# A recurrent mixer's scan in stages between the weight tiles of the next pair's products, with its GpSimd work on other engines

## The chip, the cores and the metric

The kernel runs on one core of one Trainium2 chip. The core has five engines that work side by side, each through its own queue in order: TensorE (PE in the profile, its weight loads PEld), VectorE (DVE), ScalarE (ACT), GpSimd (POOL) and SyncE (SP), which here only issues DMAs. The metric is the device time of one execution in microseconds (us); lower is better.

## The reference

One layer of a decoder with 256 tokens and a width of 2048, in float32: half a SwiGLU step, a token mixer with two branches (attention and a gated linear recurrence, HGRN2), and another half SwiGLU step. Only the recurrent branch is touched here:

```python
def hgrn2_branch(hq, hf, hi, hg, lower_bound, out_norm, w_o):
    q = heads(jax.nn.silu(hq), HGRN_EXPAND)
    f_gate = lb + (1.0 - lb) * jax.nn.sigmoid(hf)
    k = heads(1.0 - f_gate, HGRN_EXPAND)
    log_f = heads(jnp.log(f_gate), HGRN_EXPAND)
    v = heads(hi, HGRN_HEAD_DIM)
    ...
    def step(state, inp):            # a chunk of 64 tokens
        qc, kc, vc, gc = inp
        b = jnp.cumsum(gc, axis=2)
        inter = jnp.einsum('bhtk,bhkv->bhtv', qc * jnp.exp(b), state)
        ...
        scores = jnp.einsum('bhtk,bhtsk,bhsk->bhts', qc, decay, kc)
        intra = jnp.einsum('bhts,bhsv->bhtv', scores, vc)
        ...
        return new_state, inter + intra
    ...
    o = rmsnorm(o, out_norm) * jax.nn.silu(hg)
    return o @ w_o
```

The decay between tokens s and t is the product of the forget gates f from s+1 to t, in each of 128 features; there are 16 heads of 128 features.

## The kernel before

The time goes into matrix products with large weights. Weights come from memory in tiles of 128x1024 (`fetch`, L81), all on SP's queue. `load_w` (L86) makes two parts of each, a rounded one `whi` (ACT, L95) and the rest `wlo` (DVE, L96), so that products of float32 come out as sums of fast ones. There are four buffers each of `raw`, `whi` and `wlo`, so both engines may work up to four tiles ahead of PE. `gemm_t` (L99) gives 256 columns transposed and takes 16 products from a tile (L111 to L115, alternately 512 and 256 columns wide); `gemm_n` (L130) gives 512 columns by tokens and takes 12 products from a tile (L126 to L128, each 512 wide).

The recurrent mixer, `hgrn` (L599 on), works on eight pairs of heads. For each pair `pair_in` (L623) makes q, f and k from two products of four tiles each, and `values_in` or `gates_in` (L653, L660) makes, for two pairs at a time, the values or the output gates from a product of eight tiles. So a pair has sixteen weight tiles. Beside them stands the `scan` (L673) of the pair before. It replaces the chunked recurrence by doubling: `pre` holds products of f from the start of a block, `suf` products to the end of a block, and `double` (L705) makes blocks twice as long, `suf` on POOL (L706) and `pre` on DVE (L707). At block lengths 8, 16, 32 and 64 the scores between the two halves of a block are a small product (L741, two a level) of A = q x pre (L735) and B = k x suf (L737), both from DVE; blocks of 8 are done at once, with reciprocals (L719, L720) and the products of L728. Masked copies on DVE (L711) or copies on ACT (L747, L748) put the scores into `sT`. A last product (L754) couples the two halves of the tokens. `heads_out` (L759) multiplies scores and values (L764 to L766), norms and gates the result, and `merge` (L782) turns it (L785) and splits it into `ob`, the operand of the branch's output product.

The tile framework's scheduler sets the order on each engine. It takes the instructions in the order in which the program writes them, by readiness and its own estimates, and writes a fixed queue for each engine; within a queue nothing overtakes. The program writes a whole scan in one piece behind the last product of the next pair, `heads_out` and `merge` at two points of the pair after that (`step` at L640 and L642). After the last pair two products of the branch's output gate, `gate_b` (`fill`, L818, L820), stand between the last scans and outputs; the other six follow, one ahead of each output product.

Of the kernel before, what the change touches and what calls it, by code (L numbers as in the profile page):

```python
# [37 lines left out]
# Where the next operand's transposes stand in program order, along the product that runs beside them (see gemm_n), and  # L38
# by how many instructions the rest of that operand's chain is put ahead; columns of the residual at a time.
# [21 lines left out]
class Ops:  # L61
    """Pools and the pieces that the stages share."""
# [36 lines left out]
    def gemm_t(self, w, act, kt):  # L99
        """256 weight columns, result transposed: a bank for 128 columns, [column, token] in two addends."""  # L100
        nc = self.nc
        ps = self.mm.tile([P, 2, 512], F32, name="mm")
        for g in range(kt // 4):
            hi, lo = self.load_w(w[g])
            for i in range(4):
                k = g * 4 + i
                for j in range(2):
# [5 lines left out]
                    else:  # L113
                        nc.tensor.matmul(ps[:, j, 0:T], lo[:, c], both[:, 0], start=False, stop=False)  # L114
                        nc.tensor.matmul(ps[:, j], hi[:, c], both, start=False, stop=k == kt - 1)  # L115
# [14 lines left out]
    def gemm_n(self, w, act, kt, n=512, late=0, pool=None, own=0, hooks=()):  # L130
# [15 lines left out]
        for g in range(kt // kg):  # L146
# [3 lines left out]
            for i in range(kg):  # L150
# [21 lines left out]
    def rstd_of(self, ssq, n, width, half=False):  # L172
        """ssq [P, n] sums of squares -> 1 / sqrt(mean + eps), or half of it."""
# [20 lines left out]
    def transposed(self, src, act, c, tt):  # L194
        """split(transpose(src)) into the k-tiles 4c.. of act."""
# [10 lines left out]
    def prenorm(self, x, ssq, wname, act, tt, ws=None):  # L206
        """act = split(transpose(x * rstd * w)) for half of the tokens."""
# [10 lines left out]
    def weighted(self, ps, c, z, wname):  # L218
        """z = y * w, a quarter of the columns."""
# [3 lines left out]
    def residual(self, x, z, rstd, done):  # L223
        """x += rstd * z, some of the columns at a time."""
# [43 lines left out]
def layer_kernel(ctx, tc, a, out):  # L268
# [9 lines left out]
    def ffn(n, act, fp, x_src, x_dst, nxt, hooks=()):  # L278
# [3 lines left out]
        # the first columns by halves of the tokens  # L282
# [62 lines left out]
    def gate_b(c):  # L345
        pg = ops.gemm_t(a["w_gb"][c], h, KD)
# [17 lines left out]
    with tc.tile_pool(name="hgrn", bufs=1, reuse_waits="tile") as gp:  # L364
        hgrn(ops, gp, h, ob, lambda i: gts.append(gate_b(i)))
    with tc.tile_pool(name="mg", bufs=1, side="right", reuse_waits="tile") as mgp:
        mg = mgp.tile([P, 2, KD, T], F32R, name="mg")
# [531 lines left out]
```

## Time and profile before

| | us |
|---|---|
| time, median of 3 runs | 2565.45 (2565.07 to 2565.91) |
| the profiled execution, first to last instruction | 2564.2 |
| in which DVE is busy | 1477.7 |
| in which ACT is busy | 1186.9 |
| in which POOL is busy | 181.1 |
| POOL in six pairs of the recurrent mixer, 1210 to 1520 | 94.4 |

No other time of the profiled execution is given than its span. The mixer's first scan begins at about 1200 us, the last output is merged at about 1560 us. A row of the profile that groups instructions gives the line, the engine, what is written from what, the shape, the count, the busy time in all and the mean of one in ns, then the idle time before them with what ended it. In the profile the operand h of these products goes by the name `after`. A float32 product that is not split counts as two instructions (L741 stands as x4 for the two products of a level).

### The profile page before, as it was taken

Reading aid. Unit: us, or ns where it says so; the run is one execution under the profiler, and the core shown is the slowest. Engines: PE = TensorE matmul, PEld = TensorE weight load, DVE = VectorE, ACT = ScalarE, POOL = GpSimd, SP = SyncE. Lnnn points to the kernel's source line nnn. Section 1 sums busy time; section 2 is a strip of 40 time slices with the busy share of each in tenths; the row PEclk is TensorE's granted clock in tenths of the full one; section 3 lists DMA queues with packets and bytes.
Section 4 is the critical chain, followed back from the end, with each engine's and each line's share of the span. In section 5 each row is a group of like instructions: output and inputs, shape, how many; then the busy total and the mean of one; then the engine's idle time right before and its main releaser. Section 6 shows DMA issues by size and latency. Waiting matters only on the chain.

```text
span 2564.2 us, 33907 instructions
## 1 busy us (share of the span) xinstructions
PE 2521.4 (98%) x13316; PEld 2147.1 (84%) x13316; DVE 1477.7 (58%) x1732; ACT 1186.9 (46%) x1552; POOL 181.1 (7%) x181
## 2 busy tenths in 40 slices
PE   8999999999999999999999999999999999999998
PEld 6888888888878898888888888888788888888887
DVE  5555555544466666556777776555655555554444
ACT  5444444434344556444444444444544444443433
POOL 0000000000000100111323231120000000000000
PEclk9999999999999999999999999999999999999999
DMA  7555555556686444555545444567755555555655
GB/s 255 174 188 189 188 183 190 188 188 199 201 271 188 162 140 148 188 181 181 165 163 169 161 157 158 188 205 242 231 175 188 187 186 188 189 189 188 197 195 184
DMA packets 137248, 481.13 MB, mean 188 GB/s; under 512 B 15616, under 2 KB 16000, under 8 KB 136320
## 3 DMA queue, kind: packets, MB, share of 16 engines
q1 hardware_dynamic: 137088, 478.97, 57.3%
q8 instruction: 104, 1.70, 0.3%
q14 instruction: 56, 0.46, 0.1%
HBM read 472.61 MB, written 6.29 MB: 187 GB/s over the span
## 4 chain that ended last, share of the span: by engine, by line
PE 93%; DVE 3%; POOL 1%; issue 1%; DMA 1%; ACT 1%; SPq 0%; POOLq 0%; DVEq 0%; ACTq 0%
PE mm L115 34%; PE mm L114 18%; PE mm L126 11%; PE mm L127 11%; PE mm L128 11%; PE mm L111 2%; PE mm L112 1%; POOL suf L706 1%; PE tp L198 0%; DVE sT L711 0%; PE sp L534 0%; PE sp L533 0%; DVE wlo L96 0%; PE sp L728 0%; PE tp L565 0%
## 5 line engine op out<-in xcount | busy, mean ns | idle before, releaser
L96 DVE TENSOR_TENSOR wlo<-raw,whi 128x1024 fp32r<-128x1024 f32 x826 | 1024.8, 1243 | 763.5 <-ACT whi L95 762.3
L95 ACT CAST whi<-raw 128x1024 fp32r<-128x1024 f32 x826 | 865.7, 1050 | 891.2 <-PE mm L115 425.3
L115 PE MATMUL mm<-h,whi 128*128 128x512 f32 x2400 | 846.0, 393 | 0.0
L114 PE MATMUL mm<-h,wlo 128*128 128x256 f32 x2400 | 678.1, 283 | 0.0
L115 PEld LDWEIGHTS mm<-h,whi 128*128 128x128 f32 x2400 | 450.7, 188 | 100.7
L114 PEld LDWEIGHTS mm<-h,wlo 128*128 128x128 f32 x2400 | 451.2, 188 | 3.8
L115 PE MATMUL mm<-after,whi 128*128 128x512 f32 x960 | 340.1, 394 | 0.0
L114 PE MATMUL mm<-after,wlo 128*128 128x256 f32 x960 | 273.1, 284 | 0.0
L127 PE MATMUL mm<-wlo,at 128*128 128x512 f32 x664 | 262.0, 395 | 0.0
L126 PE MATMUL mm<-whi,at 128*128 128x512 f32 x664 | 262.0, 395 | 0.0
L128 PE MATMUL mm<-whi,at 128*128 128x512 f32 x664 | 261.7, 395 | 0.0
L115 PEld LDWEIGHTS mm<-after,whi 128*128 128x128 f32 x960 | 180.4, 188 | 38.9
L114 PEld LDWEIGHTS mm<-after,wlo 128*128 128x128 f32 x960 | 180.6, 188 | 1.2
L126 PEld LDWEIGHTS mm<-whi,at 128*128 128x128 f32 x664 | 125.1, 188 | 29.2
L128 PEld LDWEIGHTS mm<-whi,at 128*128 128x128 f32 x664 | 125.1, 188 | 29.2
L127 PEld LDWEIGHTS mm<-wlo,at 128*128 128x128 f32 x664 | 125.1, 188 | 29.2
L178 POOL TENSOR_TENSOR rs<-ms,mhalf 128x1 f32<-128x1 f32 x16 | 9.7, 605 | 1633.3 <-DVE ms L176 1633.3
L126 PE MATMUL mm<-whi,after 128*128 128x512 f32 x304 | 120.9, 398 | 1.2 <-ACT after L164 1.2
L128 PE MATMUL mm<-whi,after 128*128 128x512 f32 x304 | 120.1, 395 | 0.0
L127 PE MATMUL mm<-wlo,after 128*128 128x512 f32 x304 | 120.0, 395 | 0.0
L115 PE MATMUL mm<-oa,whi 128*128 128x512 f32 x240 | 84.6, 393 | 0.0
L115 PE MATMUL mm<-ob,whi 128*128 128x512 f32 x240 | 84.6, 393 | 0.0
(276 smaller groups left out, 2860.9 us busy)
## 6 DMA issues: line engine op xcount, KB each, us to landing
raw<-in_ffn_w_gate SPq DMA_DIRECT2D x176, 512.0 KB, 4.3
raw<-in_ffn_w_up SPq DMA_DIRECT2D x176, 512.0 KB, 3.5
raw<-in_ffn_w_down SPq DMA_DIRECT2D x176, 512.0 KB, 4.3
raw<-in_w_ga SPq DMA_DIRECT2D x32, 512.0 KB, 3.4
raw<-in_mla_w_o SPq DMA_DIRECT2D x32, 512.0 KB, 3.6
raw<-in_w_hq SPq DMA_DIRECT2D x32, 512.0 KB, 3.6
raw<-in_w_hf SPq DMA_DIRECT2D x32, 512.0 KB, 3.5
raw<-in_w_hi SPq DMA_DIRECT2D x32, 512.0 KB, 3.5
```

The source lines that it names most:

```text
L95: nc.scalar.copy(out=hi, in_=raw)
L96: nc.vector.tensor_tensor(out=lo, in0=raw, in1=hi.bitcast(F32), op=ALU.subtract)
L111: nc.tensor.matmul(ps[:, j], hi[:, c], both, start=True, stop=False)
L112: nc.tensor.matmul(ps[:, j, 0:T], lo[:, c], both[:, 0], start=False, stop=False)
L114: nc.tensor.matmul(ps[:, j, 0:T], lo[:, c], both[:, 0], start=False, stop=False)
L115: nc.tensor.matmul(ps[:, j], hi[:, c], both, start=False, stop=k == kt - 1)
L126: nc.tensor.matmul(o, both[:, 0, r], hi[:, c], start=k == 0, stop=False)
L127: nc.tensor.matmul(o, both[:, 0, r], lo[:, c], start=False, stop=False)
L128: nc.tensor.matmul(o, both[:, 1, r], hi[:, c], start=False, stop=k == kt - 1)
L178: self.nc.gpsimd.tensor_tensor(out=r, in0=ms, in1=self.mhalf[:, 0:n], op=ALU.pow)
L706: G.tensor_tensor(out=part(suf, n, True), in0=part(suf, n, True), in1=ends(pre, n, False), op=ALU.mult)
```

## The change

The scan becomes a generator of eight stages, the outputs one of two. `gemm_t` and `gemm_n` call `tick` after each weight tile, and `tick` runs the stages that `lay` has planned for this place: those of a scan after every second tile of the next pair's sixteen, from the second tile on; those of the outputs after the third and the sixth. The last scan has one stage after each tile of the first two output gates, of which the mixer now takes three (`fill(2)`), so that five follow.

Each stage first issues the score products whose operands the stage before has made, then DVE's work for the next level. A and B of a level are made for both halves of the tokens by one operation each (before: two). POOL's operations move: `suf` goes to DVE, its first doubling as a copy to ACT; f = lb1 x sigmoid + lb and k = 1 - f go to ACT, the clamp of f to DVE. The norm's weight is no longer multiplied into the gates, but into the merge, where it is a scalar for each partition. The last doubling makes only the halves that are used.

```diff
-    def gemm_t(self, w, act, kt):
+    def gemm_t(self, w, act, kt, tick=None):
...
+            if tick:
+                tick()
...
     def pair_in(pr, tick):
...
         for j in range(2):
             c = slice(2 * pr + j, 2 * pr + j + 1)
-            G.tensor_scalar(out=f[:, :, j], in0=sf[:, :, j], scalar1=lb1[:, c], scalar2=lb[:, c], op0=ALU.mult,
-                            op1=ALU.add)
+            S.activation(out=f[:, :, j], in_=sf[:, :, j], func=AF.Identity, scale=lb1[:, c], bias=lb[:, c])
-        G.tensor_scalar(out=k, in0=f, scalar1=-1.0, scalar2=1.0, op0=ALU.mult, op1=ALU.add)
-        G.tensor_scalar(out=f, in0=f, scalar1=F_MIN, scalar2=None, op0=ALU.max)
+        S.activation(out=k, in_=f, func=AF.Copy, scale=-1.0, bias=1.0)
+        V.tensor_scalar(out=f, in0=f, scalar1=F_MIN, scalar2=None, op0=ALU.max)
...
     def gates_in(g, tick):
...
-        G.tensor_tensor(out=gv, in0=gv, in1=onw.unsqueeze(1).broadcast_to([P, 8, P]), op=ALU.mult)
...
         def double(n):
-            G.tensor_tensor(out=part(suf, n, True), in0=part(suf, n, True), in1=ends(pre, n, False), op=ALU.mult)
-            V.tensor_tensor(out=part(pre, n, False), in0=part(pre, n, False), in1=ends(pre, n, True), op=ALU.mult)
+            es, ls = (slice(0, 1), slice(1, 2)) if 2 * n == P else (slice(0, 2), slice(0, 2))
+            if n == 1:
+                S.copy(out=part(suf, n, True), in_=ends(pre, n, False))
+            else:
+                V.tensor_tensor(out=part(suf, n, True)[:, es], in0=part(suf, n, True)[:, es],
+                                in1=ends(pre, n, False)[:, es], op=ALU.mult)
+            V.tensor_tensor(out=part(pre, n, False)[:, ls], in0=part(pre, n, False)[:, ls],
+                            in1=ends(pre, n, True)[:, ls], op=ALU.mult)
...
         double(1)
         double(2)
+        yield
...
-        pick(0, ps)
-        double(4)
         for i, n in enumerate(LEVELS):
...
-            for tt in range(NT):
-                V.tensor_tensor(out=placed(A, n, tt, False), in0=halves(q, n, tt, False), in1=halves(pre, n, tt, False),
-                                op=ALU.mult)
-                V.tensor_tensor(out=placed(B, n, tt, True), in0=halves(k, n, tt, True), in1=halves(suf, n, tt, True),
-                                op=ALU.mult)
+            V.tensor_tensor(out=placed(A, n, False), in0=part(q, n, False), in1=part(pre, n, False), op=ALU.mult)
+            V.tensor_tensor(out=placed(B, n, True), in0=part(k, n, True), in1=part(suf, n, True), op=ALU.mult)
+            if i == 0:
+                pick(0, ps)
+            double(n)
+            yield
             ps = sp.tile([P, 2, 2, P], F32, name="sp")
...
-            double(n)
...
-            ops.split(ob[:, 0, 2 * pr:2 * pr + 2], ob[:, 1, 2 * pr:2 * pr + 2], o)
+        S.activation(out=hi, in_=o, func=AF.Copy, scale=onw)
+        V.scalar_tensor_tensor(out=lo, in0=o, scalar=onw, in1=hi.bitcast(F32), op0=ALU.mult, op1=ALU.subtract)
...
+    plan, left = [], []
+
+    def tick():
+        if plan:
+            for stage in plan.pop(0):
+                next(stage, None)
+
+    def lay(pairs):
+        for first, apart, gen in pairs:
+            for i in range(8 if gen.__name__ == "scan" else 2):
+                while len(plan) <= first + i * apart:
+                    plan.append([])
+                plan[first + i * apart].append(gen)
...
     for pr in range(8):
+        if pr > 1:
+            lay([(2, 3, outputs(*left.pop(0)))])
+        if pr:
+            lay([(1, 2, scanned(*pend))])
...
+    lay([(1, 2, outputs(*left.pop(0))), (0, 1, scanned(*pend))])
+    fill(0, tick)
+    fill(1, tick)
+    lay([(0, 2, outputs(*left.pop(0)))])
+    fill(2, tick)
```

The queues show what this moves. First PE's, before, where the scan of the third pair begins (L728 are the scores in blocks of 8, L741 those of a level, L111 and L112 the next pair's products):

```order
L128 MATMUL mm<-whi,after_4283 128x512
L728 MATMUL sp<-A_10937,B_10938 128x128 x4
L741 MATMUL sp<-A,B 128x128 x2
L111 MATMUL mm<-after_4283,whi 128x512
L112 MATMUL mm<-after_4283,wlo 128x256
L111 MATMUL mm<-after_4283,whi 128x512
L741 MATMUL sp<-A,B 128x128 x2
L112 MATMUL mm<-after_4283,wlo 128x256
```

The two first levels have three products between them, the next two come after 17 and 10 more, and the last small product (L754) after another 10; so the scan lies within the first product of a pair. The same place of the changed kernel, with the lines of that kernel (L735 for L728, L747 for L741, L792 the turn of the outputs, L116 and L117 for L114 and L115):

```order
L117 MATMUL mm<-after_4283,whi 128x512
L792 MATMUL tp<-ident,xn 128x128 x4
L735 MATMUL sp<-A_10661,B_10662 128x128 x4
L116 MATMUL mm<-after_4283,wlo 128x256
L117 MATMUL mm<-after_4283,whi 128x512
L116 MATMUL mm<-after_4283,wlo 128x256
```

Here 32 products stand between L735 and the first L747, and 24 from each small product to the next, so the scan lies over the whole pair.

Next DVE, before, behind the first reciprocal of the same scan (L735 and L737 are A and B, L707 is `pre`, L96 a weight tile's rest):

```order
L720 RECIPROCAL tmp<-f 128x2x32x4
L96 TENSOR_TENSOR wlo<-raw,whi 128x1024
L721 TENSOR_TENSOR A_10937<-q,tmp 128x2x32x4
L96 TENSOR_TENSOR wlo<-raw,whi 128x1024
L722 TENSOR_TENSOR A_10937<-q,f 128x2x32x4
L724 TENSOR_TENSOR B_10938<-k,tmp 128x2x32x4
L707 TENSOR_TENSOR f<-f 128x2x32x4
L737 TENSOR_TENSOR B<-k,suf 128x16x8
L735 TENSOR_TENSOR A<-q,f 128x16x8
L96 TENSOR_TENSOR wlo<-raw,whi 128x1024
L735 TENSOR_TENSOR A<-q,f 128x16x8
L737 TENSOR_TENSOR B<-k,suf 128x16x8
```

And now (L708 is `suf`, L710 `pre`, L739 and L740 are A and B):

```order
L725 RECIPROCAL tmp<-f 128x2x32x4
L96 TENSOR_TENSOR wlo<-raw,whi 128x1024
L726 TENSOR_TENSOR A_10661<-q,tmp 128x2x32x4
L728 TENSOR_TENSOR B_10662<-k,suf 128x2x32x4
L727 TENSOR_TENSOR A_10661<-q,f 128x2x32x4
L96 TENSOR_TENSOR wlo<-raw,whi 128x1024
L729 TENSOR_TENSOR B_10662<-k,tmp 128x2x32x4
L708 TENSOR_TENSOR suf<-suf,f 128x2x32x4
L710 TENSOR_TENSOR f<-f 128x2x32x4
L740 TENSOR_TENSOR B<-k,suf 128x2x16x8
L739 TENSOR_TENSOR A<-q,f 128x2x16x8
L96 TENSOR_TENSOR wlo<-raw,whi 128x1024
```

`suf` stands among DVE's own operations, and A and B of a level are one operation each. Ahead of these rows stand three doublings (L710, L708, L710) and the first reciprocal behind one wlo; behind them come six more scan operations (L708, L710, L740, L739, L708, L710), in every other pair the gate's product with them, and four wlo with hardly anything between.

Last the tail on DVE, in the last scan (L715 is a masked copy, L125 adds up an output gate, L796 is the merge):

```order
L715 COPY_PREDICATED sT<-masks,sp 128x512
L96 TENSOR_TENSOR wlo<-raw,whi 128x1024
L125 TENSOR_TENSOR gb<-gb,mm 128x512
L796 SCALAR_TENSOR_TENSOR ob<-tp,onw,ob 128x512
L715 COPY_PREDICATED sT<-masks,sp 128x512
L739 TENSOR_TENSOR A<-q,f 128x2x4x32
L740 TENSOR_TENSOR B<-k,suf 128x2x4x32
L96 TENSOR_TENSOR wlo<-raw,whi 128x1024
L715 COPY_PREDICATED sT<-masks,sp 128x512
L708 TENSOR_TENSOR suf<-suf,f 128x2x4x32
L96 TENSOR_TENSOR wlo<-raw,whi 128x1024
L710 TENSOR_TENSOR f<-f 128x2x4x32
```

Two operations of the outputs (L786, 128x256) stand ahead of these rows behind the same wlo; B and A of level 64 follow them, and on PE that level's product stands one tile earlier. One stage a tile is laid here instead of one in two.

More of the change, by code (lines that the diff above doesn't have):

```diff
@@ L128, in _tok, with gemm_n @@
         nc.tensor.matmul(o, both[:, 1, r], hi[:, c], start=False, stop=k == kt - 1)
-    def gemm_n(self, w, act, kt, n=512, late=0, pool=None, own=0, hooks=()):
+    def gemm_n(self, w, act, kt, n=512, late=0, pool=None, own=0, hooks=(), tick=None):
         kg = 1024 // n
@@ L604, in hgrn @@
     nc.sync.dma_start(out=masks, in_=a["hmask"])
-    onw = gp.tile([P, P], F32, name="onw")
-    nc.sync.dma_start(out=onw, in_=a["hgrn_out_norm"].broadcast_to([P, P]))
+    onw = gp.tile([P, 1], F32, name="onw")
+    nc.sync.dma_start(out=onw, in_=a["hgrn_out_norm"])
     lg = gp.tile([P, 2, NH], F32, name="lg")
@@ L639, in pair_in @@
         sf = tmp()
-        step(1)
-        total(sf, ops.gemm_t(a["w_hf"][pr], h, KD))
-        step(1)
+        total(sf, ops.gemm_t(a["w_hf"][pr], h, KD, tick))
         S.activation(out=sf, in_=sf, func=AF.Sigmoid)
@@ L671, in view, with scan @@
         return bass.AP(t.tensor, t.offset + start, [list(t.ap[0])] + [list(d) for d in dims])
-    def scan(pr, q, f, k, four):
+    def scan(pr, q, f, k, box):
         pre = f
@@ L782, in merge @@
-        def merge(on):
-            pt = tp.tile([P, 4, P], F32, name="tp")
-            for u in range(4):
-                nc.tensor.transpose(out=pt[:, u], in_=on[:, u], identity=ident)
-            o = pt.rearrange("p (j t) b -> p j (t b)", j=2)
-            ops.split(ob[:, 0, 2 * pr:2 * pr + 2], ob[:, 1, 2 * pr:2 * pr + 2], o)
-        return heads_out, merge
-    later = []
-    def step(n):
-        for _ in range(n):
-            if later:
-                later.pop(0)()
-    def out_of(fns, later):
-        heads_out, merge = fns
+        v, gt = four
@@ new lines, in outputs @@
+        po = tp.tile([P, 4, P], F32, name="tp")
+        for j in range(2):
+            hs = slice((head + j) * P, (head + j + 1) * P)
+            nc.tensor.matmul(po[:, 2 * j], sT[:, 0, j], v[:, 0, hs], start=True, stop=True)
+            nc.tensor.matmul(po[:, 2 * j + 1], sT[:, 1, j], v[:, 1, hs], start=True, stop=False)
+            nc.tensor.matmul(po[:, 2 * j + 1], cT[:, j], v[:, 0, hs], start=False, stop=True)
+        ssq = small.tile([P, 4], F32, name="ossq")
+        for u in range(4):
+            ops.square_sum(ssq[:, u:u + 1], po[:, u])
@@ new lines, in outputs @@
+        ms = small.tile([P, 4], F32, name="oms")
+        G.tensor_scalar(out=ms, in0=ssq, scalar1=1.0 / P, scalar2=EPS, op0=ALU.mult, op1=ALU.add)
+        rstd = small.tile([P, 4], F32, name="ors")
+        G.tensor_tensor(out=rstd, in0=ms, in1=ops.mhalf[:, 0:4], op=ALU.pow)
+        on = small.tile([P, 4, P], F32, name="xn", bufs=2)
+        for u in range(4):
+            S.activation(out=on[:, u], in_=po[:, u], func=AF.Copy, scale=rstd[:, u:u + 1])
+        for j in range(2):
+            V.tensor_tensor(out=on[:, 2 * j:2 * j + 2], in0=on[:, 2 * j:2 * j + 2],
+                            in1=gt[:, :, (head + j) * P:(head + j + 1) * P], op=ALU.mult)
@@ new lines, in outputs @@
+        yield
+        pt = tp.tile([P, 4, P], F32, name="tp")
+        for u in range(4):
+            nc.tensor.transpose(out=pt[:, u], in_=on[:, u], identity=ident)
+        o = pt.rearrange("p (j t) b -> p j (t b)", j=2)
+        hi, lo = (ob[:, i, 2 * pr:2 * pr + 2] for i in range(2))
+        S.activation(out=hi, in_=o, func=AF.Copy, scale=onw)
[5 more added lines that the diff above has]
+                next(stage, None)
@@ L801, in out_of, with scanned @@
+    def lay(pairs):
[4 more added lines that the diff above has]
+                plan[first + i * apart].append(gen)
+    def scanned(pr, q, f, k, four):
         box = []
-        later.append(lambda: box.append(heads_out()))
-        later.append(lambda: merge(box[0]))
+        left.append((pr, box, four))
+        return scan(pr, q, f, k, box)
@@ L805, in hgrn @@
     pend = None
     for pr in range(8):
-        new = pair_in(pr, step)
+        if pr > 1:
+            lay([(2, 3, outputs(*left.pop(0)))])
+        if pr:
+            lay([(1, 2, scanned(*pend))])
+        new = pair_in(pr, tick)
         if pr % 2 == 0:
-            four = [values_in(pr // 2)]
+            four = [values_in(pr // 2, tick)]
         else:
-            four.append(gates_in(pr // 2))
-        new += (four,)
-        if pend is not None:
-            out_of(scan(*pend), later)
@@ L815, in hgrn @@
-        pend = new
-    step(2)
-    out_of(scan(*pend), later)
-    fill(0)
-    step(1)
-    fill(1)
-    step(1)
+            four.append(gates_in(pr // 2, tick))
+        pend = new + (four,)
+    lay([(1, 2, outputs(*left.pop(0))), (0, 1, scanned(*pend))])
[3 more added lines that the diff above has]
+    fill(2, tick)
 def _tiles(w, cols, group):
```

64 lines of the change are left out of this document (23 added, 41 removed).

## Prediction

> **What bounds the kernel now.** I read the page's busy times first, then PE's own waits, then the busy times by stretch through the recurrent mixer, and last the order of time around one wait.
>
> ```profile
> span 2564.2 us, 33907 instructions
> PE 2521.4 (98%) x13316; PEld 2147.1 (84%) x13316; DVE 1477.7 (58%) x1732; ACT 1186.9 (46%) x1552; POOL 181.1 (7%) x181
> ```
>
> PE is busy for 98% of the span and the change keeps every one of its products. So the most that a reordering can win is PE's idle time, and of that only the part that lies in the mixer. PE's waits say which part that is (waiter, what it waited for, us in total, times, longest):
>
> ```profile
> PE tp L198 <- DVE xn L214: 16.4, 5, 9.7
> PE sp L741 <- DVE B L737: 8.4, 11, 1.4
> ...
> PE sp L754 <- DVE q L750: 1.4, 5, 0.3
> ...
> PE tp L764 <- ACT sT L747: 0.8, 1, 0.8
> PE tp L785 <- DVE xn L778: 0.7, 1, 0.7
> ...
> PE tp L766 <- ACT cT L755: 0.5, 1, 0.5
> ```
>
> The 16.4 us on top belong to the norms between the big stages (L198, L214), which the change does not touch. The other five rows are the scan and its outputs: 8.4 + 1.4 + 0.8 + 0.7 + 0.5 = 11.8 us in 19 waits. The busy times by stretch, one pair of heads each and the tail last, place them:
>
> ```profile
> core 0: us, PE busy (x) PEld busy (x) DVE busy (x) ACT busy (x) POOL busy (x), PEclk, DMA share, GB/s
> 1210.00:1262.80 52.80, 50.61 (x271) 42.78 (x270) 38.78 (x57) 24.24 (x42) 16.77 (x16) 1.00 0.50 160
> 1262.80:1313.50 50.70, 50.25 (x270) 42.53 (x269) 35.95 (x56) 24.23 (x41) 14.67 (x15) 1.00 0.52 166
> 1313.50:1366.10 52.60, 50.42 (x270) 42.58 (x270) 38.76 (x57) 24.25 (x41) 16.74 (x16) 1.00 0.48 161
> 1366.10:1416.80 50.70, 50.26 (x270) 42.53 (x270) 35.97 (x56) 24.22 (x41) 14.65 (x15) 1.00 0.51 166
> 1416.80:1469.40 52.60, 50.45 (x271) 42.61 (x270) 38.77 (x57) 24.24 (x41) 16.73 (x16) 1.00 0.50 160
> 1469.40:1520.30 50.90, 50.30 (x271) 42.59 (x270) 36.05 (x56) 24.23 (x41) 14.79 (x15) 1.00 0.52 166
> 1520.30:1560.00 39.70, 35.53 (x222) 29.97 (x221) 32.87 (x65) 20.17 (x52) 14.08 (x15) 1.00 0.33 107
> ```
>
> PE idles 2.19, 0.45, 2.18, 0.44, 2.15 and 0.60 us in the six pairs and 4.17 us in the tail: 12.2 us, which is the 11.8 us again. All idle stands here, the clock is full, DMA is half loaded, and DVE, the busiest of the others, has 12 to 15 us free in each pair. So it is a matter of order, not of load. One wait in order of time (start, us, engine and line, idle before it and who ended it):
>
> ```profile
> 1213.00 2.41 POOL L667 TENSOR_TENSOR hg<-hg,onw 128x1024 f32<-128x1024 f32 x1 [10.24 <-DVE hg L665]
> ...
> 1213.48 2.08 DVE L735 TENSOR_TENSOR A<-q,f 128x128 f32<-128x128 f32 x1
> ...
> 1215.13 0.39 PE L115 MATMUL mm<-after,whi 128*128 128x512 f32 x1
> 1215.48 0.71 DVE L711 COPY_PREDICATED sT<-masks,sp 128x512 f32<-128x512 int32 x1
> ...
> 1216.92 1.49 POOL L706 TENSOR_TENSOR suf<-suf,f 128x256 f32<-128x256 f32 x1 [1.50 <-DVE B L737]
> 1216.92 0.68 PE L741 MATMUL sp<-A,B 128*128 128x128 f32 x4 [1.41 <-DVE B L737]
> ```
>
> DVE's A (L735; its twin L737 takes 0.28, below) takes 2.08 us while POOL multiplies the gate weights, and with nothing but program order between them PE stands from 1215.13 to 1216.92 for the level's operands. Between these starts lie 1.79 us, where two products of this size follow each other after 0.23 us (below); the row counts only 1.41 us of it, since a busy row of 0.39 us hides 0.16 us of each wait. So 19 waits are worth 12.2 + 19 x 0.16 = **15.2 us**, and this is the pot.
>
> **The change, part by part.** *Order on PE.* The scan's products stand 24 or 32 products apart instead of 3 to 17. What that gives is read from the distance to DVE, by the weight tiles (a tile's cast, its rest, the next tile's):
>
> ```profile
> 1204.62 1.05 ACT L95 CAST whi<-raw 128x1024 fp32r<-128x1024 f32 x1 [1.74 <-PE mm L128]
> 1205.71 1.23 DVE L96 TENSOR_TENSOR wlo<-raw,whi 128x1024 fp32r<-128x1024 f32 x1 [1.35 <-ACT whi L95]
> ...
> 1207.41 1.05 ACT L95 CAST whi<-raw 128x1024 fp32r<-128x1024 f32 x1 [1.74 <-PE mm L128]
> ...
> 1208.49 1.23 DVE L96 TENSOR_TENSOR wlo<-raw,whi 128x1024 fp32r<-128x1024 f32 x1 [1.56 <-ACT whi L95]
> ```
>
> A tile lasts 2.79 us (1204.62 to 1207.41; 12 products of 512 columns, so 0.23 each). There are four buffers, so a cast starts when PE leaves the tile four before; DVE has the rest ready 2.31 us later (1207.41 to 1209.72), and PE wants it after three more tiles, 8.37 us. DVE may therefore be **6.1 us late** before PE waits for a weight tile, and each tile leaves it 2.79 - 1.22 = 1.57 us for scan work. In the new order a level's A and B stand on DVE, counted in tiles, two to eight places ahead of PE's product, each place another 2.79 us on top of the 6.1; only in the tail do they stand level with it or one place behind. Within the pairs a score product thus waits only if DVE has used up all that.
>
> *Work on DVE.* Rows of the six pairs, 1210 to 1520:
>
> ```profile
> L96 DVE TENSOR_TENSOR wlo<-raw,whi 128x1024 fp32r<-128x1024 f32 x96 | 116.5, 1219 | 31.8 <-ACT whi L95 31.4
> L735 DVE TENSOR_TENSOR A<-q,f 128x128 f32<-128x128 f32 x48 | 18.5, 395 | 0.0
> L707 DVE TENSOR_TENSOR f<-f 128x256 f32<-128x256 f32 x42 | 17.8, 424 | 27.2 <-POOL suf L706 27.2
> L737 DVE TENSOR_TENSOR B<-k,suf 128x128 f32<-128x128 f32 x48 | 13.5, 282 | 0.0
> ...
> L719 DVE RECIPROCAL tmp<-suf 128x256 f32<-128x256 f32 x6 | 10.5, 1746 | 0.0
> ...
> L721 DVE TENSOR_TENSOR A<-q,tmp 128x256 f32<-128x256 f32 x6 | 5.0, 827 | 0.0
> ...
> L637 DVE TENSOR_TENSOR q<-q,tmp 128x512 f32<-128x512 f32 x6 | 4.1, 684 | 0.0
> ...
> L722 DVE TENSOR_TENSOR A<-q,f 128x256 f32<-128x256 f32 x6 | 2.5, 418 | 0.0
> ```
>
> For each pair sixteen A and B go ((18.5 + 13.5) / 6 = 5.33 us) and eight of twice the size come (8 x 0.418 = 3.34). Six products of suf come from POOL: five of 0.424 and a half one of about 0.28, 2.40 us; half of the last pre goes, 0.14. The clamp of f comes too, a one-input operation that no row shows: between 0.28 (L737, a quarter of its elements) and 0.68 us (L637, its size with two inputs); I take 0.5. The norm weight in the merge costs at most 0.1. Sum: -5.33 + 3.34 + 2.40 - 0.14 + 0.5 + 0.1 = +0.9, so DVE has 39.7 us of work in a pair of 50. Its 27.2 us of waiting for POOL's suf go.
>
> The densest stretch is the one with the reciprocals, shown above. Between one wlo and the next stand 3 x 0.42 + 1.75 = 3.0; 1.75; 3 x 0.42 = 1.3; 5 x 0.42 = 2.1; 6 x 0.42 = 2.5 us: 10.6 us against 5 x 1.57 = 7.9. DVE falls 2.8 us behind, 4.0 with the gate's product (1.2 us, in every other pair), under 6.1. It costs nothing, and four bare tiles follow. The added waits are the mask copies (L715), which wait for a score product of PE; behind them on DVE stands the next wlo. In the order a copy stands two or three tile places after its product. At two, DVE comes to it 2.31 us after PE began the tile before the product, which ends at 2.79 + 0.45: 0.9 us of waiting, off the 6.1 us and not off PE (4.0 + 0.9 = 4.9).
>
> *Work on ACT and POOL.*
>
> ```profile
> L643 ACT ACTIVATE tmp<-tmp 128x512 f32<-128x512 f32 x6 | 3.9, 644 | 0.0
> ...
> L755 ACT COPY cT<-sp 128x256 f32<-128x256 f32 x6 | 2.2, 374 | 3.7 <-PE sp L754 3.6
> ```
>
> ```profile
> L706 POOL TENSOR_TENSOR suf<-suf,f 128x256 f32<-128x256 f32 x42 | 45.1, 1074 | 142.8 <-DVE B L737 86.0 <-DVE tmp L719 53.1 <-DVE f L707 3.2
> L650 POOL TENSOR_SCALAR f<-f 128x512 f32<-128x512 f32 x6 | 14.1, 2342 | 0.5
> ...
> L667 POOL TENSOR_TENSOR hg<-hg,onw 128x1024 f32<-128x1024 f32 x3 | 7.2, 2407 | 30.3 <-DVE hg L665 30.3
> ```
>
> ACT gets two halves of f, k and the first suf: 2 x 0.37 + 0.64 + 0.37 = 1.8 us on 24.2 of 50; covered. If it were not, a cast would come later and eat the same 6.1 us. POOL keeps two memsets and the norm's two small steps. The memset of suf waits for the old pair's last read, and ACT's copy and DVE's first doubling wait for it; in DVE's order this stands seven tiles before PE's first score product, so it is covered as well.
>
> The trace shows POOL and DVE in each other's way: POOL's suf took 1.49 us beside a wlo above, 1.07 on average, and DVE's L721 takes 0.83 us where L722, of the same shape, takes 0.42. The Trainium skill (SBUF — State Buffer, Who interferes with whom) states that a VectorE instruction with two SBUF inputs and a GpSimd one that reads SBUF take turns, the second waiting for the whole of the first. By that rule the 0.4 us of each L721 and the long A go as well, 0.6 us a pair off DVE; without it DVE has 39.7 us. The sum on PE is 15.2 us either way.
>
> *The tail.* The last scan has one tile a stage. From the wlo before its first mask copy DVE has 2 x 0.42 + 0.73, then 0.68 + 0.68 + 0.73 + 2 x 0.42, then 0.73 + 0.42 us between the next three tiles: 5.7 us against 3 x 1.57, so 1.0 late. Level 64's doubling, A and B (3 x 0.42 = 1.3 us) then stand one place behind their product on PE: 6.1 - 2.8 - 1.0 - 1.3 leaves 1.0 us of spare. That is thin: nothing is left at best, 2 us of waiting if each stage runs half a microsecond longer; I take 0.5. The DMAs keep their order on SP but for one load of 128x1 in place of 128x128; nothing hangs on it.
>
> *Sum:* 15.2 - 0.5 = 14.7 us. The span becomes 2564.2 - 14.7 = 2549.5; the median before, 2565.45, is 1.25 us over the profiled span, which I carry over: **2550.7 us**, 0.6% less.
>
> **The rivals.** *Part of it stays.* If DVE's stretches run 6 to 8 us late in the odd pairs and the tail, each of four places costs 1 to 2 us: 5 to 8 us stay, 2555.7 to 2558.7 us. For it: the thin spare in the tail. Against: the 1.2 us and more in the pairs.
>
> *The wait moves.* The mask copies wait for PE with a wlo behind them, and PE waits for that wlo: were they in step, a wait of up to 1.4 us (the longest of L741 now) would stand at two levels of each pair, 8 x 2 x 0.9 = 14 us back: 2565 us, no change. Against it: the 6.1 us.
>
> *Slower: DVE becomes the bound.* A pair now has 27 operations of 128x256 on DVE. If their strided or backward views cost what L721 costs, 0.83 for 0.42 us, that is 11 us more, 50.7 us a pair against PE's 49.5 (below): DVE decides from there. At 0.92 us each it is 53.2 us, and 8 x 3.7 = 30 us are lost against 15 won: 2580 us. Against it: L707 and L722 have such views at 0.42.
>
> **How the numbers follow.** (A small product's time is from this row, (1.05 - 0.16) / 8 = 0.11 us.)
>
> ```profile
> 1210.00 1.05 PE L728 MATMUL sp<-A,B 128*128 128x128 f32 x8
> ```
>
> The forecast has a chance of 0.79, part of it 0.12, the moved wait 0.05, DVE as the bound 0.04. The bounds of the pot: six pairs take 1520.3 - 1210.0 = 310.3 us, and 6 x (16 tiles of 2.79 us + 44 small products of 0.11 us) would take 297, 49.5 a pair; with 5 us in the tail (4.17 idle, the rest hidden) that is 18 us, so 2547 us is the low end. The high end takes in half of the second case: 2557 us. A measurement of this kernel tells about 0.2%, 5.1 us, from no change: faster 0.91, same 0.05, slower 0.04.
>
> **What would show it.** Right: PE's waits for A, B, q and k gone from the list, stretches of a pair near 49.8 us with PE idle under 0.5, DVE 38 to 40 us in each, POOL under 5 us, the rest of the program unmoved. Wrong: PE waiting for a wlo (DVE late), operations of 128x256 above 0.5 us, or a score product still waiting in the last pair. The prediction fails as a whole if DVE's stretches run over 6.1 us late.

## The result and the profile after

The changed kernel takes **2547.07 us** (median of 4 runs, 2545.72 to 2547.95) where the kernel before, run beside it, takes 2565.37 (2565.07 to 2565.91): a ratio of 0.9927, 95% interval 0.9915 to 0.9940. That is 18.3 us less, at the very low end of the predicted range (2547 us), where 14.7 were forecast. The profiled execution has a span of 2546.2 us, 18.0 under the one before. The page begins:

```profile
span 2546.2 us, 33763 instructions
...
PE 2515.4 (99%) x13316; PEld 2148.7 (84%) x13316; DVE 1482.0 (58%) x1724; ACT 1202.6 (47%) x1584; POOL 75.7 (3%) x89
```

PE has the same 13316 instructions and DVE about the same busy time; POOL lost 105 of its 181 us. PE's own waits after (waiter, what it waited for, us in total, times, longest) begin like this:

```profile
PE tp L204 <- DVE xn L220: 16.8, 5, 10.8
PE tp L514 <- POOL xn L468: 1.9, 4, 0.8
PE mm L130 <- ACT after L170: 1.2, 2, 0.8
...
PE mm L131 <- DVE wpair L96: 0.2, 1, 0.2
```

Not one row of the scan or its outputs is left: the 11.8 us in 19 waits are gone, and no wait for a weight tile's `wlo` has come in their place. The rows of the norms (L204, L198 before) stand as they were. The busy times by stretch, cut where the first score product of each pair starts, the tail last:

```profile
core 0: us, PE busy (x) PEld busy (x) DVE busy (x) ACT busy (x) POOL busy (x), PEclk, DMA share, GB/s
1232.80:1282.47 49.67, 49.67 (x270) 42.64 (x269) 37.39 (x56) 26.28 (x45) 2.26 (x4) 1.00 0.52 170
1282.47:1332.15 49.68, 49.68 (x271) 42.65 (x269) 38.37 (x57) 26.28 (x45) 2.25 (x4) 1.00 0.52 170
...
1481.19:1522.45 41.26, 41.26 (x223) 35.30 (x221) 32.78 (x50) 21.19 (x36) 1.56 (x3) 1.00 0.55 181
1522.45:1560.00 37.55, 37.55 (x234) 33.48 (x234) 23.39 (x34) 21.83 (x43) 1.36 (x3) 1.00 0.46 155
```

Every pair now takes 49.68 us, where pairs of 52.6 and 50.7 us alternated before, and PE has no idle time in any of them or in the tail. DVE's groups in five pairs, 1232 to 1481 us:

```profile
L715 DVE COPY_PREDICATED sT<-masks,sp 128x512 f32<-128x512 int32 x15 | 11.1, 737 | 6.7 <-PE sp L747 6.7
...
L708 DVE TENSOR_TENSOR suf<-suf,f 128x256 f32<-128x256 f32 (+1 forms) x30 | 12.0, 399 | 0.5
...
L740 DVE TENSOR_TENSOR B<-k,suf 128x256 f32<-128x256 f32 x20 | 8.4, 420 | 0.0
...
L653 DVE TENSOR_SCALAR f<-f 128x512 f32<-128x512 f32 x5 | 2.1, 419 | 0.0
...
L726 DVE TENSOR_TENSOR A<-q,tmp 128x256 f32<-128x256 f32 x5 | 2.1, 413 | 0.0
```

The mask copies (L715) wait for PE, 6.7 us in five pairs or 1.3 us a pair, and that reaches nobody. It is no longer than before, in six pairs; only the product waited for is another:

```profile
L711 DVE COPY_PREDICATED sT<-masks,sp 128x512 f32<-128x512 int32 x18 | 13.2, 733 | 8.1 <-PE sp L728 8.1
```

**Where 18 us come from, when PE idled for only 12.2.** Two places are the same in both programs: the first product of the mixer and the first turn behind the norm after it. In order of time, before:

```profile
1120.45 0.39 PE L111 MATMUL mm<-after,whi 128*128 128x512 f32 x1
...
1805.14 0.66 PE L198 MATMUL tp<-ident,xn 128*128 128x128 f32 x4 [0.95 <-DVE xn L214]
```

and after:

```profile
1121.78 0.39 PE L113 MATMUL mm<-after,whi 128*128 128x512 f32 x1
...
1787.49 0.66 PE L204 MATMUL tp<-ident,xn 128*128 128x128 f32 x4 [0.94 <-DVE xn L220]
```

Between them lie 684.69 us before and 665.71 after. The mixer gained 19.0 us; 1.3 us were lost ahead of it, 1.1 of them at the first norm of the program, whose longest wait was 9.7 and is 10.8 here (9.5 to 10.8 in the runs below, so a difference between executions). I counted the 19.0 us in the starts of PE's rows, where a product of 512 columns is followed after 0.23 us and one of 256 after 0.12. Whatever a small product starts later than that is a wait: 10.5 us before in the six pairs and 4.9 in the tail, **15.4 us** in all, and none after. The remaining 3.6 us are in the small products themselves (counted directly they take 3.9 less, the large ones about 0.2 more). The score product between the halves of the tokens, before, with the row behind it:

```profile
1222.56 0.68 PE L754 MATMUL sp<-q,k 128*128 128x128 f32 x4 [0.31 <-DVE q L750]
1223.00 0.36 PE L114 MATMUL mm<-after,wlo 128*128 128x256 f32 x1
```

and the same product between the same neighbours in experiment 5 below, where its operands are there in time:

```profile
1220.20 0.60 PE L750 MATMUL sp<-q,k 128*128 128x128 f32 x4
1220.56 0.36 PE L114 MATMUL mm<-after,wlo 128*128 128x256 f32 x1
```

From start to start it lasts 0.44 us where it had to wait and 0.36 where it had not. So a late operand costs 0.08 us more than the wait, in a row that counts as busy. The first weight loads of the two (PEld) show what differs:

```profile
1222.53 0.52 PEld L754 LDWEIGHTS sp<-q,k 128*128 128x128 f32 x4 [0.60 <-issue]
...
1220.07 0.54 PEld L750 LDWEIGHTS sp<-q,k 128*128 128x128 f32 x4
```

The load that had to wait begins 0.03 us ahead of its product, the other 0.13 us ahead, beside the large product in front of it. All groups of four small products between large ones in the mixer fall in two kinds so: a load at most 0.05 us ahead goes with 0.42 us or more, one at least 0.11 us ahead with 0.35 or 0.36. Before, 33 of 41 groups are of the first kind, after none. At least seven of the 33 start in time and are long all the same: at the second level of a scan the load waits for the mask copy L711 behind the first one, and not for an operand.

Over the mixer the small products take 38.3 us before (27.7 in the six pairs, 10.6 in the tail) and 34.4 after. About 0.6 of the 3.9 us between them is one plain wait inside a run of small products in the tail (at 1552.45 us, 0.46 of it idle by the profile); the late loads go with the other 3.2.

### The profile page after: what moved, and what is told of

Same layout as the page of the kernel before. It is cut to its first block, busy times and chain, and to the rows that moved or that the text cites. A ratio compares the mean times of both kernels' runs of the same rounds, so it can differ in the third digit from the quotient of the medians.

```text
span 2546.2 us, 33763 instructions
## 1 busy us (share of the span) xinstructions
PE 2515.4 (99%) x13316; PEld 2148.7 (84%) x13316; DVE 1482.0 (58%) x1724; ACT 1202.6 (47%) x1584; POOL 75.7 (3%) x89
## 4 chain that ended last, share of the span: by engine, by line
PE 96%; DVE 1%; DMA 1%; ACT 1%; POOL 0%; issue 0%; SPq 0%; POOLq 0%; DVEq 0%; ACTq 0%
PE mm L117 36%; PE mm L116 18%; PE mm L130 11%; PE mm L131 11%; PE mm L132 11%; PE mm L113 3%; PE mm L114 1%; PE sp L747 1%; DMA raw<-in_ffn_w_gate 0%; PE tp L204 0%; PE sp L540 0%; PE sp L539 0%; DVE wlo L96 0%; PE sp L735 0%; PE tp L571 0%
## 5 line engine op out<-in xcount | busy, mean ns | idle before, releaser
L96 DVE TENSOR_TENSOR wlo<-raw,whi 128x1024 fp32r<-128x1024 f32 x826 | 1025.1, 1242 | 765.6 <-ACT whi L95 763.9
L117 PE MATMUL mm<-h,whi 128*128 128x512 f32 x2400 | 846.0, 394 | 0.0
L116 PE MATMUL mm<-h,wlo 128*128 128x256 f32 x2400 | 678.4, 283 | 0.0
L117 PEld LDWEIGHTS mm<-h,whi 128*128 128x128 f32 x2400 | 451.1, 188 | 100.5
L116 PEld LDWEIGHTS mm<-h,wlo 128*128 128x128 f32 x2400 | 451.3, 188 | 3.8
L117 PE MATMUL mm<-after,whi 128*128 128x512 f32 x960 | 339.5, 394 | 0.0
L116 PE MATMUL mm<-after,wlo 128*128 128x256 f32 x960 | 273.2, 285 | 0.0
L130 PE MATMUL mm<-whi,at 128*128 128x512 f32 x664 | 262.1, 395 | 0.0
L117 PEld LDWEIGHTS mm<-after,whi 128*128 128x128 f32 x960 | 180.5, 188 | 39.3
L116 PEld LDWEIGHTS mm<-after,wlo 128*128 128x128 f32 x960 | 180.6, 188 | 1.5
L130 PEld LDWEIGHTS mm<-whi,at 128*128 128x128 f32 x664 | 125.2, 188 | 29.1
L130 PE MATMUL mm<-whi,after 128*128 128x512 f32 x304 | 122.8, 404 | 1.2 <-ACT after L170 1.2
L117 PE MATMUL mm<-oa,whi 128*128 128x512 f32 x240 | 84.6, 394 | 0.0
L117 PE MATMUL mm<-ob,whi 128*128 128x512 f32 x240 | 84.6, 394 | 0.0
L124 ACT COPY m<-mm 128x512 f32<-128x512 f32 x56 | 32.8, 586 | 97.1 <-PE mm L117 97.1
```

The source lines that it names most:

```text
L96: nc.vector.tensor_tensor(out=lo, in0=raw, in1=hi.bitcast(F32), op=ALU.subtract)
L124: self.nc.scalar.copy(out=out, in_=ps[:, :, T:512])
L130: nc.tensor.matmul(o, both[:, 0, r], hi[:, c], start=k == 0, stop=False)
```

## The experiments

The two halves of the change, the order on PE and the moves off POOL, were taken apart first. The times of the kernel before beside these runs are medians of 2566.3 to 2566.6 us. Lines in the diffs and profiles are each kernel's own.

**1. The order alone**: the changed kernel with all of POOL's work back on POOL (f, k, the clamp, `suf`, the norm weight in the gates). A and B stay merged into one operation a level.

```diff
-            S.activation(out=f[:, :, j], in_=sf[:, :, j], func=AF.Identity, scale=lb1[:, c], bias=lb[:, c])
+            G.tensor_scalar(out=f[:, :, j], in0=sf[:, :, j], scalar1=lb1[:, c], scalar2=lb[:, c], op0=ALU.mult,
+                            op1=ALU.add)
...
+        G.tensor_tensor(out=gv, in0=gv, in1=onw.unsqueeze(1).broadcast_to([P, 8, P]), op=ALU.mult)
...
-                V.tensor_tensor(out=part(suf, n, True)[:, es], in0=part(suf, n, True)[:, es],
-                                in1=ends(pre, n, False)[:, es], op=ALU.mult)
+            G.tensor_tensor(out=part(suf, n, True)[:, es], in0=part(suf, n, True)[:, es],
+                            in1=ends(pre, n, False)[:, es], op=ALU.mult)
```

> The changed kernel's stages and its queue on PE, with all the work of f, k, the clamp, suf and the gates' norm weight back on POOL. Theory (the order makes the gain: a score product that stands two tiles behind its operands waits for nobody): PE's waits in the mixer stay under 3 us, all of them in the last scan, and the time is 2547 to 2551 us. Rival (the gain is POOL's work and the turns it takes with DVE): PE waits 8 us or more in the mixer and the time is 2555 us or more.

Measured: 2546.91 us, ratio 0.9926 (0.9911 to 0.9941). Pairs of 49.68 us, and no row of the scan among PE's waits. The order with the merged A and B is enough for the whole gain; the moves add nothing to the time that can be measured. What they add is spare: in the rows of both engines a weight tile's first product here starts as little as 0.9 us after the end of its `wlo` (at 1169.6 us, ahead of the first scan) and 3.3 us in the pairs; in the changed kernel it is 4.4 and 5.5 us.

**2 to 4. Each move alone**, in the kernel before, its scan in one piece. Experiment 2 moves the norm weight from POOL's product of the gates into the merge:

```diff
-        G.tensor_tensor(out=gv, in0=gv, in1=onw.unsqueeze(1).broadcast_to([P, 8, P]), op=ALU.mult)
...
-            ops.split(ob[:, 0, 2 * pr:2 * pr + 2], ob[:, 1, 2 * pr:2 * pr + 2], o)
...
+            S.activation(out=hi, in_=o, func=AF.Copy, scale=onw)
+            V.scalar_tensor_tensor(out=lo, in0=o, scalar=onw, in1=hi.bitcast(F32), op0=ALU.mult, op1=ALU.subtract)
```

> The kernel before with one part of the change: the norm's weight goes from POOL's product with the gates (2.4 us, every other pair) into the merge. PE's queue stays as before. If that product makes DVE's A late (2.08 us) and so the long wait of every other pair, these pairs lose 1.5 to 1.9 of their 2.2 us of idle: 4 to 7 us less, 2559 to 2562 us. If suf alone makes the waits, nothing changes: 2564 to 2566 us.

Measured: 2559.25 us, ratio 0.9971 (0.9960 to 0.9982). Stretches of two pairs (columns as above), then PE's waits:

```profile
1210.11:1260.91 50.80, 50.17 (x269) 42.56 (x268) 37.01 (x57) 24.32 (x41) 15.73 (x15) 1.00 0.51 165
1260.91:1311.70 50.79, 50.36 (x270) 42.60 (x269) 35.98 (x56) 24.34 (x41) 16.06 (x15) 1.00 0.51 166
```

```profile
PE sp L739 <- DVE B L735: 2.3, 7, 0.3
...
PE sp L752 <- DVE q L748: 1.4, 5, 0.3
```

The long pair of 52.6 us has become a short one; the waits of 1.4 us are gone, those of up to 0.3 stay. So the long wait of every other pair is POOL's product of the gates beside DVE's A. Experiment 3 moves `suf` alone to DVE (the first doubling to ACT, the last one halved, of `pre` as well):

```diff
-            G.tensor_tensor(out=part(suf, n, True), in0=part(suf, n, True), in1=ends(pre, n, False), op=ALU.mult)
...
+            if n == 1:
+                S.copy(out=part(suf, n, True), in_=ends(pre, n, False))
+            else:
+                V.tensor_tensor(out=part(suf, n, True)[:, es], in0=part(suf, n, True)[:, es],
+                                in1=ends(pre, n, False)[:, es], op=ALU.mult)
...
```

> The kernel before with one part of the change: suf from POOL to DVE (its first doubling to ACT, the last one halved). If POOL's suf, 1.5 us a level between one level's B and the next, makes the waits, nearly all go: 2549 to 2553 us. If the gates' product makes those of every other pair, 5 to 8 us stay: 2555 to 2559 us.

Measured: 2556.78 us, ratio 0.9962 (0.9947 to 0.9977):

```profile
1211.08:1262.57 51.49, 50.11 (x270) 42.63 (x269) 40.70 (x63) 24.68 (x42) 9.40 (x9) 1.00 0.50 164
1262.57:1312.41 49.84, 49.84 (x269) 42.60 (x268) 37.87 (x62) 24.67 (x42) 7.00 (x8) 1.00 0.52 169
```

```profile
PE sp L748 <- DVE B L744: 5.6, 4, 1.4
```

The other way round: the short pair has lost its waits, and the four long waits, one in every other pair, are what is left. Experiment 4 moves f, k and the clamp alone, to ACT and DVE:

```diff
...
-        G.tensor_scalar(out=k, in0=f, scalar1=-1.0, scalar2=1.0, op0=ALU.mult, op1=ALU.add)
-        G.tensor_scalar(out=f, in0=f, scalar1=F_MIN, scalar2=None, op0=ALU.max)
+        S.activation(out=k, in_=f, func=AF.Copy, scale=-1.0, bias=1.0)
+        V.tensor_scalar(out=f, in0=f, scalar1=F_MIN, scalar2=None, op0=ALU.max)
```

> The kernel before with one part of the change: f and k on ACT, the clamp on DVE. They stand in a part of the pair where PE does not wait, so nothing changes: 2564 to 2566 us. If POOL's queue as a whole is what is late (4.7 us of it go), the waits shrink by half: 2557 us or less.

Measured: 2566.18 us, ratio 0.9999 (0.9990 to 1.0008). It does nothing to the time.

**5. All moves together, without the order**: the three edits above and the merged A and B in the kernel before.

> The kernel before with the scan in one piece as it was, and only the moves between engines: f, k on ACT, clamp and suf on DVE, A and B merged, the norm weight in the merge. Theory (order): the products of a level still stand a few products behind their operands, so most of the 18 us of stall stays; a level's chain is shorter without POOL's 1.5 us, which gives 3 to 8 us: 2557 to 2562 us. Rival (moves): 2551 us or less.

Measured: 2550.61 us, ratio 0.9943 (0.9926 to 0.9959), a miss: I had expected the moves to leave most of the waits. A stretch of one pair and one over the tail, and the longest of PE's waits there:

```profile
1210.44:1260.14 49.70, 49.70 (x270) 42.59 (x269) 38.29 (x56) 26.19 (x45) 2.27 (x4) 1.00 0.51 169
1509.00:1560.00 51.00, 49.40 (x309) 43.52 (x308) 41.08 (x69) 28.64 (x62) 3.01 (x5) 1.00 0.42 141
```

```profile
PE tp L781 <- DVE xn L774: 1.3, 1, 1.3
```

The moves alone also clear the pairs, by the other way: with the chain on one engine, DVE keeps up with score products that stand close behind each other. The gains of experiments 2 to 4 (7.0, 9.5 and 0.1 us) add up to 16.6, this one is 15.8. What the order has over it is in the tail, where PE idles 1.6 us here. Between the two places used above, the mixer lasts 668.9 us here and 665.7 in experiment 1; by the starts of PE's rows about 2.4 of these 3.2 us are waits and 1.0 longer small products. The merged A and B were not run alone, and both this kernel and experiment 1 have them.

**6. `suf` alone back on POOL** in the changed kernel (the last edit shown for experiment 1).

> The changed kernel with suf alone back on POOL. Theory (order): POOL's 1.5 us a doubling fits into a stage of 5.6 us, PE waits only in the last scan if at all: 2547 to 2550 us. Rival (POOL and DVE in turns): DVE's operations of 128x256 take up to 0.8 us again, DVE's time in a pair rises from 38 to over 42 us, PE waits, and the time is 2552 us or more.

Measured: 2547.39 us, ratio 0.9929 (0.9914 to 0.9944), pairs of 49.68 us. With the operands a tile or two early it does not matter where `suf` is made.

**7 and 8. How much slack the order leaves.** First the stages of a scan one tile apart and not two:

```diff
-            lay([(1, 2, scanned(*pend))])
+            lay([(1, 1, scanned(*pend))])
```

> The changed kernel with a scan's eight stages one tile apart instead of two, within the first half of a pair. If a stage's 2.4 us on DVE against 1.57 us a tile makes DVE late, as the forecast reckoned (0.85 us a stage, on top of 2.8 us for the reciprocals, against a spare of 6.1), PE waits 2 to 4 us in each pair: 2560 to 2575 us. If the spare is hardly touched, because DVE works ahead wherever its inputs are there, under 1 us in all: 2546 to 2549 us.

Measured: 2546.99 us, ratio 0.9924 (0.9907 to 0.9941):

```profile
1232.00:1281.65 49.65, 49.65 (x269) 42.62 (x268) 36.81 (x56) 26.27 (x45) 2.27 (x4) 1.00 0.52 170
```

No wait appears: half the distance does. Then three buffers for `whi` and `wlo` in place of four:

```diff
-            hi = self.wp.tile([P, 1024], F32R, name="whi", bufs=4)
-            lo = self.wp.tile([P, 1024], F32R, name="wlo", bufs=4)
+            hi = self.wp.tile([P, 1024], F32R, name="whi", bufs=3)
+            lo = self.wp.tile([P, 1024], F32R, name="wlo", bufs=3)
```

> The changed kernel with three buffers of the weights' two parts in place of four. Theory (DVE may be late by its distance to PE, 6.1 us, and is up to 4.9 us late): the distance falls to 3.3 us, so PE waits for a weight tile, 1.6 us in every other pair, 0.4 us in the others and 2 us in the tail: 6 to 9 us more in the mixer. Rival (DVE is hardly ever late; the spare was never used): under 1.5 us more in the mixer. The big products outside the mixer may lose as well; that is read apart.

Measured: 2560.54 us, ratio 0.9978 (0.9969 to 0.9987) to the kernel before, 13.5 us over the changed one. A pair, and then the first of PE's waits:

```profile
1238.87:1288.55 49.68, 49.68 (x271) 42.63 (x270) 37.38 (x55) 26.27 (x46) 2.26 (x4) 1.00 0.50 170
```

```profile
PE tp L204 <- DVE xn L220: 23.6, 6, 9.9
PE mm L130 <- ACT wpair L95: 2.0, 1, 2.0
```

The mixer's pairs lose nothing. Most of the loss is at the norms between the big stages (23.6 us in place of 16.8, 6 us more at one norm ahead of the mixer), the rest mainly at the products behind the last scan (L130) and not in it. One buffer less takes a tile, 2.79 us, off the 6.1 us that DVE may be late. With 4.9 us of lateness, as forecast, PE would have had to wait; so DVE is less than 3.3 us late in the pairs.

**9 to 12. From which load on DVE decides.** Work whose result nobody reads is added on DVE in each scan. In 9 and 10 it is a reciprocal of a tile of ones per stage, of 128x256 or 128x128:

```diff
+                if stage.__name__ == "scan":
+                    for _ in range(1):
+                        V.reciprocal(out=ones[:, 0], in_=ones[:, 0])
```

> The changed kernel with one reciprocal of 128x256 more on DVE behind each of a scan's eight stages, which nobody reads: 8 x 1.75 = 14 us a pair. DVE's 38 us in a pair become 52 against PE's 49.7. If DVE becomes the bound there, as the third rival of the forecast has it, a pair takes 52 us: 7 x 2.3 us and up to 8 us in the last scan, 2560 to 2572 us. If DVE may run late without PE waiting (products far behind their operands), less than 5 us: below 2552 us.

> The same with reciprocals of 128x128: 8 x 0.9 = 7 us a pair, DVE 45 us of 49.7. If what counts is DVE's load in a pair, PE waits for nothing but perhaps in the last scan: 2546 to 2550 us. If the stretch with the reciprocals of the scan was near its limit, as the forecast reckoned (4.9 of 6.1 us), PE waits 1 to 3 us a pair: 2555 us or more.

Measured: 2546.80 us, ratio 0.9924 (0.9908 to 0.9941), and 2546.82 us, ratio 0.9924 (0.9909 to 0.9938). They settle less than was meant: since these reciprocals wait for nothing of the scan, the scheduler put nearly all of them ahead of the loaded stretch (of the large ones 49 before 1232 us, 16 in the next two pairs). Of the first kernel one of those two pairs:

```profile
1232.02:1281.70 49.68, 49.68 (x270) 42.67 (x268) 48.11 (x63) 26.28 (x45) 2.49 (x4) 1.00 0.51 170
```

DVE is busy for 48.1 of 49.7 us there and PE still does not wait. For 11 the work is tied to the scan, one reciprocal of `pre` ahead of each of its seven yields, 7 x 1.75 = 12.2 us a pair:

```diff
+        V.reciprocal(out=dump[:, 0], in_=pre[:, 0])
         yield
```

> The load of e9 bound to its place: one reciprocal of 128x256 more, of the running products, behind each of a scan's seven steps, read by nobody; 7 x 1.75 = 12.2 us a pair, so that DVE has 38 + 12 = 50 us in a pair of 49.7. If DVE's load decides, a pair takes about 50 us: 0.5 us more each, 3 to 8 us with the last scan, 2549 to 2556 us. If the dense stretches decide first (the forecast's 4.9 of 6.1 us), PE waits 3 us or more a pair: 2568 us or more.

Measured: 2554.70 us, ratio 0.9956 (0.9940 to 0.9973):

```profile
1232.18:1282.13 49.95, 49.94 (x270) 42.63 (x269) 48.60 (x64) 26.24 (x46) 2.50 (x4) 1.00 0.50 169
1282.13:1331.81 49.68, 49.68 (x270) 42.65 (x269) 47.23 (x63) 26.36 (x46) 3.03 (x4) 1.00 0.52 170
```

```profile
PE mm L113 <- ACT whi L95: 1.6, 1, 1.6
PE tp L778 <- ACT sT L758: 1.4, 1, 1.4
...
PE mm L116 <- DVE wlo L96: 0.7, 1, 0.7
...
PE mm L114 <- DVE wlo L96: 0.6, 1, 0.6
```

By the sum DVE has about 50 us of work a pair; the rows count it as busy for 48.6 and 47.2. The pairs begin to stretch by a quarter of a microsecond or less in every other one; the rest of the loss is waits in the last scan (1527 to 1541 us), which has one tile a stage. 12 adds a second reciprocal of 128x128 in the same places, 18.9 us a pair in all.

> As e11, with one of 128x128 more at each of the seven places: 7 x (1.75 + 0.95) = 18.9 us a pair, DVE 57 us. If DVE is the bound from there, as the third rival says, each of seven pairs takes 57 us, 7.3 us more, and the last scan some 15 more: 2605 to 2620 us. If the products behind the scan give it room that the sum of a pair does not show, under 2580 us.

Measured: 2604.10 us (one run, so no interval):

```profile
1232.29:1289.55 57.26, 52.66 (x271) 44.03 (x269) 54.73 (x72) 26.49 (x46) 2.27 (x4) 0.97 0.45 147
1289.55:1345.11 55.56, 51.89 (x271) 43.99 (x269) 52.14 (x69) 26.18 (x46) 2.57 (x4) 0.97 0.45 152
```

```profile
PE mm L131 <- DVE wlo L96: 13.7, 11, 2.0
PE tp L782 <- ACT sT L761: 8.8, 7, 1.7
```

The two pairs last 56.4 us on average, near the sum of DVE's work, 38 + 18.9 = 56.9 us, and PE waits for weight tiles and for scores (`sT`) that come late: the third rival's mechanism. By its price, eight times the excess over 49.7, that is 2547 + 8 x 7.2 = 2604.6 us. The agreement is closer than the case allows: it is one run, the rows count DVE as busy for only 54.7 and 52.1 us, and PE's granted clock is 0.97 here, its busy time 52 to 53 us in place of 49.7. How much of the stretch is the clock's was not separated. The change stands some 10 us of DVE's work a pair away from the point where the pairs stretch.

No kernel here was faster than the changed one by more than a measurement can tell.

## Why the prediction was wrong, and what in it was right

*The cause* was right. PE stood in its queue at small products whose operands DVE and POOL made in turns, and products placed a tile or two behind their operands do not wait. The experiments add that there are two cures, and that either does most of the work: distance (1) or a shorter chain (5). The forecast reckoned only with the first, which was the right one to reckon with, since the moves add nothing to it.

*The step that failed* is the size of the pot: "the most that a reordering can win is PE's idle time", and so "12.2 + 19 x 0.16 = 15.2 us". As a count of waits it was right: the starts give 15.4. But it held that the products keep their time, and the small ones do not: each whose weight load is held up also lasts longer, 0.44 in place of 0.36 us in most cases. That, with one wait inside a run of small products that the starts of the runs do not show, is the 3.6 us that were missing, 19.0 in all. The same prediction had a better reading beside it: the floor of a pair from its products, 16 tiles and 44 small products at 0.11 us, 49.5 us, which needs no idle time at all. The pairs came out at 49.68. It was used only for the low end of the range, and should have been the forecast: 18 us, 2547 us. That it met the sum so well is in part luck: it gave 13 us in the six pairs and 5 in the tail, and the six pairs gave 12.1, the rest 6.9.

*"I take 0.5" for the tail* was wrong as well, in the same direction: nothing is left there. The reckoning of DVE's lateness behind it was too dark. In the pairs it gave 4.9 of 6.1 us. In the rows of both engines a tile's first product starts in the changed kernel never less than 4.4 us after its `wlo` ends, and in the pairs of the scan and the tail never less than 5.5, so DVE was late there by no more than 0.6 us; experiments 7 and 8 fit that. The sum over stretches took each stretch's work against one tile's allowance, as though DVE could not work ahead in the bare tiles between, and took a tile as 2.79 us, while with its small products a pair gives each of its tiles 49.68 / 16 = 3.1. Which of the two weighs more was not tested. It cost nothing, since both answers lie under 6.1.

*Work on DVE*: 37.4 and 38.4 us a pair, against 39.7 forecast. The 39.7 put the 0.9 us of new work on the long pair of before (38.8); over the mean of before, 37.4, it would have been 38.3. Measured is 0.5 over that mean, and the 0.41 us that L721 lost is the difference. (The 0.6 us a pair that the prediction gave to the taking of turns does not follow from its rows: the long A was already in the 5.33 us.) The clamp took 0.42 us (0.28 to 0.68, taken as 0.5), `suf` 0.40, merged A and B 0.42; no view of 128x256 is dear. *Work on ACT* is 26.3 us a pair, covered as forecast (experiment 4). 

*The rivals.* "Part of it stays" did not happen. "The wait moves" did not: the mask copies do wait for PE, 1.3 us a pair (0.9 was reckoned for one), but no more than before, and a `wlo` 5.5 us early hides it. "DVE becomes the bound" did not, for want of load; experiments 11 and 12 fit its point of decision at 50 us and, by one run, its price.

*Taking turns.* The prediction held that L721's 0.83 us would fall to 0.42 and DVE's long A with it, by what it quotes of the Trainium skill (SBUF — State Buffer, Who interferes with whom). Both fell (L726, 0.413 above). Which POOL operation it was is in the order of time, before:

```profile
1245.27 2.34 POOL L650 TENSOR_SCALAR f<-f 128x512 f32<-128x512 f32 x1
...
1246.17 0.83 DVE L721 TENSOR_TENSOR A<-q,tmp 128x256 f32<-128x256 f32 x1
```

The clamp, then, and not `suf`. In experiment 3, where the clamp stays on POOL and `suf` goes, the groups show

```profile
L728 DVE TENSOR_TENSOR A<-q,tmp 128x256 f32<-128x256 f32 x5 | 4.1, 827 | 0.0
```

and in experiment 4, where the clamp goes and `suf` stays,

```profile
L720 DVE TENSOR_TENSOR A<-q,tmp 128x256 f32<-128x256 f32 x5 | 2.1, 419 | 0.0
```

That the two hinder each other agrees with the rule. That the second waits for the whole of the first fits DVE's A of 2.08 us, which ends at 1215.56, 0.15 us behind POOL's product of the gates; it does not fit L721, which ends at 1247.00, 0.61 us ahead of the clamp. At L721 it was worth nothing to the time: experiment 4 has it and gains 0.1 us. At the product of the gates, where PE stood for the result, it was worth up to the 7.0 us of experiment 2, which takes that product off POOL.

## What to carry to other kernels

Read what an in-order engine loses from the starts of its rows, against the floor that its own work gives for a period, and not from its idle time: idle time here was 12.2 of 19.0 us. A small dependent product is best placed a tile or two behind its operands; then it no longer matters which engine makes them, as long as the busiest helper's work in a period stays under the main engine's. Where you load an engine to find that point, tie the added work to the data of the place, or the scheduler carries it elsewhere.

## What was not expected of the hardware

A product that waited for its operand takes 0.08 us longer than the same one that did not (0.44 and 0.36 us, above), and its weight load begins 0.03 us ahead of it and not 0.13. POOL's time depends on its neighbours as well: the clamp that takes 2.34 us beside DVE's `wlo` and A takes, in experiment 1, ahead of a `wlo`,

```profile
1245.79 1.54 POOL L654 TENSOR_SCALAR f<-f 128x512 f32<-128x512 f32 x1
...
1245.90 1.62 DVE L96 TENSOR_TENSOR wlo<-raw,whi 128x1024 fp32r<-128x1024 f32 x1
```

1.54 us, and there the `wlo` behind it takes 1.62 us in place of 1.22. No run here shows the clamp undisturbed. A fourth buffer of `whi` and `wlo` is worth about 13 us, none of it in the mixer's pairs. And the granted clock of PE, 1.00 in every stretch before and after, was 0.97 in the overloaded pairs of experiment 12, where PE stood idle for 4 us in each.
